# High parts first, low parts after, and the gate loads of layer 0's second attention released from VectorE's order: a two-layer attention trunk

## The chip, the cores and the metric

The kernel runs on one core of one Trainium2 chip. The metric is the device time of one launch in microseconds, the median of three runs. Five engines work side by side, each through its own queue in order: PE (TensorE: matmuls and transposes), DVE (VectorE), ACT (ScalarE), POOL (GpSimd) and SP (SyncE, which here only issues transfers). PEld is PE's loading of weights. Lines such as L575 are line numbers of the kernel before; the changed kernel has two or three lines more above most of them, so its L577 is the same statement.

## What is computed

Two layers of a trunk with two kinds of attention side by side. 512 latent tokens and 256 context tokens, 1024 channels, heads of 64 channels. One layer, cut to what matters:

```
h    = rmsnorm(x) * (1 + scale) + shift            # scale, shift, gate from c @ w_ada
a_k, a_v, b_k, b_v, a_q, b_q, a_z, b_z, g_a, g_b = split(h @ w_in)
a    = neighbourhood_attention(norm(a_q), norm(a_k), a_v)        # 8 heads, "NA"
b    = grouped_query_attention(rope(norm(b_q)), rope(norm(b_k)), b_v)  # 8 heads, 2 of keys, "GQA"
o_a  = (a * silu(a_z)) @ w_o_a
o_b  = (b * silu(b_z)) @ w_o_b
x    = x + gate * ((sigmoid(g_a) * o_a + sigmoid(g_b) * o_b) @ w_out)
```

Both attentions also read the context's keys. Layer 0 updates the context tokens as well; layer 1, the last, does not.

## The kernel before

**Products in three terms.** Weights and activations are float32. Each is split into a high part (a rounded copy, made by ACT) and a low part (the original minus the high part, made by DVE or POOL), and every projection is high x high + low x high + high x low, three matmuls (L467 to L469). A weight's way is therefore: a load on SP (`raw`), ACT's cast (`whi`, L452), and a subtraction (`wlo`, L454) on DVE or, by turns, on POOL.

**Queries.** A block of 128 tokens of queries is projected, normalised per head (`y`, L549), and turned on PE by four transposes into a bank of PSUM (`pst`, L561). `turn` then reads the turned block twice per half: ACT writes the high part in float16, DVE the low part. The halves are the two heads of a pair (partitions 0 to 63 and 64 to 127); for the neighbourhood attention's queries (`qa`, scaled by a column of gains: L574 on ACT, L575 on DVE) the first and the fourth block are also cut in two along the tokens, so such a block has four pairs of copies and the others have two. The grouped attention's queries (`qb`) are turned without gains (L571 on ACT, L572 on DVE). In program order each pair is high, low, high, low.

**Attention.** `pipeline` goes over eight heads: scores of head h (`pss`), on DVE the sum with the bias and the maximum (L1018 for NA, L1206 for GQA), on ACT the exponential, a split of the weights into two float16 parts (`h`: ACT L895, DVE or POOL L896), a transpose by transfer on SP (`ht`, L900; for the context's own queries `ct`), then the values of head h-1 on PE (`psv`, `pst`).

**Fill.** PE's remaining work in the attention is pieces of projections from a list, `fill`: gate projections (`psf` banks, evacuated by ACT and DVE: `za` and `zt` at L667) and then the output projection of the first branch, whose activations are split into `gah` (ACT, L711) and `gal` (POOL, L712) and whose results go into `tg` by DVE (L747). The list comes from `in_order`: the loads of two chunks first, then each chunk's pieces, with the load of the chunk after next behind the first ones. In layer 0's GQA the call passes `first`, which is true in layer 0, and every later load of that list is then issued through `tied`:

```
def tied(fn):
    behind(ON_DVE, fn, latest(ON_DVE, 4))
...
fill = in_order(gates[n_na:] + o_chunks("a", prepare, evac_a), first)
```

`behind` adds orders without a semaphore: the DVE instructions that the load emits may not be placed before the last four DVE instructions emitted until then.

**What sets the order.** The program is written in one order, and a list scheduler, which simulates the engines and transfers, places each instruction on its engine. So the order of an engine's queue differs from that of the text, and a changed dependency can move things far from it.

## Time and profile before

| | |
|---|---|
| runs | 1122.0, 1124.23, 1125.29 us; median 1124.23 us |
| the profiled execution | 1119.77 us, of which the span that the profile covers is 1118.0 us |
| granted clock of PE, mean | 0.992 |
| transfers | 178.21 MB, 159 GB/s in the mean |

The profile gives each engine's busy time, groups of instructions, waits, and the instructions in order of time. A window's row lists for each engine its busy time and, in brackets, how many instructions it had, then the clock granted to PE (1.00 is full) and the share of the transfer engines. Times are microseconds from the span's start. Layer 0's query blocks of NA lie at 120 to 160 us, its NA at 160 to 300, its query blocks of GQA at 345 to 375 and its GQA at 375 to 540; layer 1's NA queries and NA lie at 745 to 868 and its GQA after that.

### The profile page before, as it was taken

What the parts mean: (1) busy time and instruction counts of PE and PEld (TensorE: products, weight loads), DVE (VectorE), ACT (ScalarE), POOL (GpSimd) and SP (SyncE); (2) the same over time, 40 slices, a digit from 0 to 9 for tenths busy, and PEclk for the clock granted to TensorE, in tenths of its full rate; (3) what the DMA queues carried; (4) which work ended last, traced back from release to release, by engine and by line L of the source; (5) the groups of instructions that cost most, each with busy time, mean ns of one, the idle gap of its engine ahead of it and who ended that gap; (6) DMA issues with size and microseconds to landing.
All of it is one profiled execution on the core that took longest, in us unless ns stands there. A gap on an engine that the chain in (4) does not pass through costs nothing.

```text
span 1118.0 us, 16953 instructions
## 1 busy us (share of the span) xinstructions
PE 1073.3 (96%) x5672; PEld 842.5 (75%) x5672; DVE 785.9 (70%) x1667; ACT 607.5 (54%) x1219; POOL 454.3 (41%) x393
## 2 busy tenths in 40 slices
PE   8999999999999999889999999999999998999898
PEld 5688877878887867666888778887766986756587
DVE  4667999975379488657576776486886775677473
ACT  6465458776433566666231275644888436688221
POOL 1044324654246155465322534332445453575421
PEclk9999999999999999989999999999999999999999
DMA  8565335654543499789533643753645537789543
GB/s 358 207 175 173 95 109 114 139 131 100 176 125 123 127 217 211 161 208 245 178 103 115 198 123 95 216 170 108 159 112 122 157 102 192 189 231 233 143 143 94
DMA packets 244463, 178.21 MB, mean 159 GB/s; under 512 B 160284, under 2 KB 210328, under 8 KB 242712
## 3 DMA queue, kind: packets, MB, share of 16 engines
q1 hardware_dynamic: 236896, 162.61, 53.6%
q0 software_dynamic: 2368, 7.87, 2.2%
q10 hardware_dynamic: 5112, 6.66, 2.1%
q8 instruction: 45, 0.74, 0.3%
q14 instruction: 42, 0.34, 0.1%
HBM read 118.86 MB, written 20.47 MB: 125 GB/s over the span
## 4 chain that ended last, share of the span: by engine, by line
PE 42%; issue 6%; DVE 6%; DMA 6%; ACT 4%; POOL 2%; SPq 1%; DVEq 0%; POOLq 0%; ACTq 0%
PE psx L468 7%; PE psx L469 7%; PE psx L467 7%; PE psf L467 5%; PE psf L468 4%; PE psf L469 4%; DMA ht<-h 3%; PE pst L1223 1%; PE pst L1224 1%; DMA rawb<-in_w_ada_dram 1%; PE pss L925 1%; PE pss L926 1%; ACT p L1207 1%; ACT h L895 1%; DVE p L1206 1%
## 5 line engine op out<-in xcount | busy, mean ns | idle before, releaser
L896 POOL TENSOR_TENSOR h<-p,h 128x256 f16<-128x256 f32 (+2 forms) x104 | 107.8, 1044 | 156.6 <-ACT h L895 106.9
L454 POOL TENSOR_TENSOR wlo<-raw,whi 128x512 fp32r<-128x512 f32 x70 | 98.5, 1415 | 118.8 <-ACT whi L452 87.6
L467 PE MATMUL psf<-hx,whi 128*128 128x512 f32 (+1 forms) x360 | 139.5, 387 | 2.8 <-DVE za L667 2.2
L469 PE MATMUL psf<-hx,wlo 128*128 128x512 f32 (+1 forms) x360 | 137.8, 383 | 0.0
L468 PE MATMUL psf<-hx,whi 128*128 128x512 f32 (+1 forms) x360 | 137.3, 381 | 0.0
L468 PE MATMUL psx<-wlo,hx 128*128 128x512 f32 (+1 forms) x328 | 120.8, 369 | 1.3 <-DVE wlo L440 1.3
L467 PE MATMUL psx<-whi,hx 128*128 128x512 f32 (+1 forms) x328 | 120.9, 370 | 0.0
L469 PE MATMUL psx<-whi,hx 128*128 128x512 f32 (+1 forms) x328 | 120.3, 367 | 0.0
L440 POOL TENSOR_TENSOR wlo<-raw,whi 128x512 fp32r<-128x512 f32 x40 | 54.4, 1362 | 136.9 <-ACT whi L437 98.4
L452 ACT CAST whi<-raw 128x512 fp32r<-128x512 f32 x136 | 81.1, 619 | 52.2 <-DMA raw<-in_w_in_dram 25.1
L437 ACT CAST whi<-raw 128x512 fp32r<-128x512 f32 x88 | 53.9, 624 | 92.1 <-PE psx L469 30.8
L540 POOL TENSOR_TENSOR ss<-ss,ehalf 128x8 f32<-128x8 f32 (+2 forms) x40 | 65.1, 1632 | 87.8 <-DVE ss L537 86.4
L1207 ACT ACTIVATE p<-pss,mx,vb 128x768 f32<-128x768 f32 x64 | 63.4, 992 | 44.8 <-DVE mx L1206 44.4
L1206 DVE CUSTOM_DVE_ANT_0 p<-pss,vb 128x768 f32<-128x768 f32 x64 | 64.3, 1013 | 31.8 <-PE pss L926 27.0
L895 ACT CAST h<-p 128x256 f16<-128x256 f32 (+2 forms) x136 | 81.6, 617 | 7.3 <-DVE p L854 2.9
L454 DVE TENSOR_TENSOR wlo<-raw,whi 128x512 fp32r<-128x512 f32 x66 | 70.8, 1079 | 20.6 <-ACT whi L452 19.3
L467 PEld LDWEIGHTS psf<-hx,whi 128*128 128x128 f32 x360 | 68.4, 190 | 15.3 <-DVE za L667 2.4
L469 PEld LDWEIGHTS psf<-hx,wlo 128*128 128x128 f32 x360 | 68.2, 189 | 12.0
L468 PEld LDWEIGHTS psf<-hx,whi 128*128 128x128 f32 x360 | 68.3, 190 | 11.3
L468 PEld LDWEIGHTS psx<-wlo,hx 128*128 128x128 f32 x328 | 62.0, 189 | 11.9 <-DVE wlo L440 2.2
L469 PE MATMUL psx<-hx,wlo 128*128 128x256 f32 (+1 forms) x208 | 69.5, 334 | 0.7 <-DVE wlo L454 0.7
L469 PEld LDWEIGHTS psx<-whi,hx 128*128 128x128 f32 x328 | 61.9, 189 | 10.1 <-DVE hx L383 0.4
(350 smaller groups left out, 2900.7 us busy)
## 6 DMA issues: line engine op xcount, KB each, us to landing
raw<-in_w_in_dram SPq DMA_DIRECT2D x168, 256.0 KB, 3.1
rawb<-in_w_ada_dram SPq DMA_DIRECT2D x48, 256.0 KB, 2.9
raw<-in_w_out_dram SPq DMA_DIRECT2D x32, 256.0 KB, 3.0
tg<-gs SPq DMA_DIRECT2D x4, 1536.0 KB, 7.3
rawx<-in_w_ada_dram SPq DMA_DIRECT2D x4, 1024.0 KB, 11.3
rawy<-in_w_ada_dram SPq DMA_DIRECT2D x4, 1024.0 KB, 10.5
gs<-zt ACTq DMA_DIRECT2D x16, 256.0 KB, 2.6
raw<-in_w_o_a_dram SPq DMA_DIRECT2D x16, 256.0 KB, 3.4
```

The source lines that it names most:

```text
L437: S.copy(hi[:, :n], raw[:, :n])
L440: e.tensor_tensor(lo[:, :n], raw[:, :n], F(hi[:, :n]), ALU.subtract)
L452: S.copy(hi, raw)
L454: lo_eng(i).tensor_tensor(lo, raw, F(hi), ALU.subtract)
L467: T.matmul(ps, lhs[0], rhs[0], start=first, stop=False)
L468: T.matmul(ps, lhs[0], rhs[1], start=False, stop=False)
L469: T.matmul(ps, lhs[1], rhs[0], start=False, stop=last)
L540: G.tensor_tensor(ss, ss, ehalf[:, :n], ALU.pow)
L895: S.copy(h[:, 0], p[:, :n])
L896: eng.tensor_tensor(h[:, 1], p[:, :n], h[:, 0], ALU.subtract)
L1206: V.tensor_tensor_reduce(p, pss, lift, gq_ndq, 3e38, ALU.add, ALU.min, mx[:, 0:1])
L1207: S.activation(p, pss, AF.Exp, bias=mx[:, 0:1], scale=gq_dq, accum_out=r[:, i:i + 1])
```

## The change

Two edits. In `turn` the low part is no longer issued right behind its high part: the subtractions are put into a list, `todo`, and issued when all the high parts of the block have been. And the call of `in_order` for the GQA's fill no longer passes `first`, so in layer 0, too, its loads are issued without `tied`.

```
+        todo = []
+
         def pair(hi, lo, x, g):
             if g is None:
                 S.copy(hi, x)
-                V.tensor_tensor(lo, x, hi, ALU.subtract)
+                todo.append(lambda: V.tensor_tensor(lo, x, hi, ALU.subtract))
             else:
                 S.activation(hi, x, AF.Copy, scale=g)
-                V.scalar_tensor_tensor(lo, x, g, hi, ALU.mult, ALU.subtract)
+                todo.append(lambda: V.scalar_tensor_tensor(lo, x, g, hi, ALU.mult, ALU.subtract))
...
                 pair(d[own], d[other], x[own], None if g is None else g[own])
+        run(todo, len(todo))
...
-            fill = in_order(gates[n_na:] + o_chunks("a", prepare, evac_a), first)
+            fill = in_order(gates[n_na:] + o_chunks("a", prepare, evac_a))
```

The instructions are the same ones and as many on every engine; only places change. Three of them follow, each before and then after. The first number in a name tells buffers apart.

DVE in layer 0's GQA, at about 392 us. Before (`mx_837` is a maximum of the context's queries, `wlo_846` and `wlo_852` are low parts of gate weights, `p_864` is the next scores' pass, `r_839` a reciprocal that PE turns next):

```order
L938 TENSOR_REDUCE mx_837_4333<-pss_836_4328 128x2
L940 TENSOR_SCALAR mx_837_4333<-mx_837_4333,vb_659_3447 128x2
L454 TENSOR_TENSOR wlo_846_4354<-raw_844_4350,whi_845_4352 128x512
L454 TENSOR_TENSOR wlo_852_4366<-raw_850_4362,whi_851_4364 128x512
L1206 ISA p_864_4487,mx_865_4488<-pss_863_4482,vb_659_3447 128x768
L1206 ISA mx_865_4488 128x1
L905 RECIPROCAL r_839_4337<-r_839_4337 128x2
L908 SCALAR_TENSOR_TENSOR zb_800_4122<-pst_889_4559,vb_659_3447,zb_800_4122 64x512
L908 SCALAR_TENSOR_TENSOR zb_800_4122<-psv_892_4583,vb_659_3447,zb_800_4122 64x256
L1206 ISA p_868_4501,mx_869_4502<-pss_867_4496,vb_659_3447 128x768
```

After:

```order
L941 TENSOR_REDUCE mx_837_4333<-pss_836_4328 128x2
L943 TENSOR_SCALAR mx_837_4333<-mx_837_4333,vb_659_3447 128x2
L1209 ISA p_864_4487,mx_865_4488<-pss_863_4482,vb_659_3447 128x768
L1209 ISA mx_865_4488 128x1
L908 RECIPROCAL r_839_4337<-r_839_4337 128x2
L454 TENSOR_TENSOR wlo_899_4606<-raw_897_4602,whi_898_4604 128x512
L911 SCALAR_TENSOR_TENSOR zb_800_4122<-pst_889_4559,vb_659_3447,zb_800_4122 64x512
L911 SCALAR_TENSOR_TENSOR zb_800_4122<-psv_892_4583,vb_659_3447,zb_800_4122 64x256
L454 TENSOR_TENSOR wlo_905_4618<-raw_903_4614,whi_904_4616 128x512
L1209 ISA p_868_4501,mx_869_4502<-pss_867_4496,vb_659_3447 128x768
```

`wlo_846` and `wlo_852` now stand 19 rows further ahead, before the first scores' pass of the stage, and the next two low parts, `wlo_899` and `wlo_905`, have come forward to this place.

DVE where the output projection of the first branch begins, at about 486 to 496 us. Before (`ho_1086` empties the bank that `psv_1123` is turned into, `tg_1053` takes in the projection's bank `psf_1055`):

```order
L908 SCALAR_TENSOR_TENSOR zb_800_4122<-pst_1120_5655,vb_659_3447,zb_800_4122 64x512
L883 TENSOR_TENSOR ho_1086_5513<-psv_1085_5504,ho_1086_5513 64x256
L908 SCALAR_TENSOR_TENSOR zb_800_4122<-psv_1123_5679,vb_659_3447,zb_800_4122 64x256
L896 TENSOR_TENSOR h_1102_5596<-p_1100_5592,h_1102_5596 128x768
L1206 ISA p_1104_5605,mx_1105_5606<-pss_1103_5600,vb_659_3447 128x768
L1206 ISA mx_1105_5606 128x1
L747 SCALAR_TENSOR_TENSOR tg_1053_5363<-tg_1053_5363,psf_1055_5367 128x512
```

After:

```order
L911 SCALAR_TENSOR_TENSOR zb_800_4122<-pst_1120_5655,vb_659_3447,zb_800_4122 64x512
L454 TENSOR_TENSOR wlo_1093_5541<-raw_1091_5537,whi_1092_5539 128x512
L1209 ISA p_1104_5605,mx_1105_5606<-pss_1103_5600,vb_659_3447 128x768
L1209 ISA mx_1105_5606 128x1
L454 TENSOR_TENSOR wlo_1131_5716<-raw_1129_5712,whi_1130_5714 128x512
L886 TENSOR_TENSOR ho_1086_5513<-psv_1085_5504,ho_1086_5513 64x256
L911 SCALAR_TENSOR_TENSOR zb_800_4122<-psv_1123_5679,vb_659_3447,zb_800_4122 64x256
L899 TENSOR_TENSOR h_1102_5596<-p_1100_5592,h_1102_5596 128x768
L1209 ISA p_1108_5618,mx_1109_5619<-pss_1107_5613,vb_659_3447 128x768
L1209 ISA mx_1109_5619 128x1
L750 SCALAR_TENSOR_TENSOR tg_1053_5363<-tg_1053_5363,psf_1055_5367 128x512
```

Two low parts that stood after the projection's first banks now stand ahead of `ho_1086`; the pass `p_1104` has come forward, and `tg_1053` stands behind one more pass, `p_1108`. On PE the scores that follow `p_1104` in the same bank (`pss_1111`) and the next ones (`pss_1115`) have come forward to stand before the second bank, `psf_1056`; on POOL `h_1081` has come forward to stand before the four `gal` subtractions.

SP at the end of layer 1's NA, at about 848 to 866 us. Before (`h_17..` up to `h_1797` are head 6's weights to be transposed, `h_1823` to `h_1838` head 7's; `raw_18..` are loads of the next stage's weights, of which three can be open at a time):

```order
L900 DMA_TRANSPOSE ht_1559_7952<-h_1782_8872 128x4x64 x2
L669 DMA gs0_87<-zt_1848_9162 128x512
L449 DMA raw_1878_9307<-in_w_in_dram 128x2x256
L435 DMA raw_1881_9313<-in_w_in_dram 128x512
L900 DMA_TRANSPOSE ht_1559_7952<-h_1787_8888 128x4x128
L900 DMA_TRANSPOSE ht_1559_7952<-h_1792_8903 128x4x128
L900 DMA_TRANSPOSE ht_1559_7952<-h_1797_8918 128x4x128
L900 DMA_TRANSPOSE ht_1559_7952<-h_1823_9026 128x4x64 x2
```

After:

```order
L993 DMA bint_1557_7946<-b_int1_84 128x256
L995 DMA bedg_1558_7947<-b_edge1_86 64x128
L672 DMA gs0_87<-zt_1846_9134 128x512
L449 DMA raw_1878_9307<-in_w_in_dram 128x2x256
L435 DMA raw_1881_9313<-in_w_in_dram 128x512
L435 DMA raw_1884_9319<-in_w_in_dram 128x512
L672 DMA gs0_87<-zt_1848_9162 128x512
L435 DMA raw_1887_9325<-in_w_in_dram 128x512
L900 DMA_TRANSPOSE ht_1559_7952<-h_1823_9026 128x4x64 x2
```

All of head 6's transposes now stand ahead of head 7's bias (`bint`, `bedg`), and two more loads, `raw_1884` and `raw_1887`, which followed head 7's transposes before, stand ahead of them.

## The prediction

> **What bounds the kernel now.** I read the page first, then windows by stage, then PE's waits in the touched stages, and last the instructions in order of time around each.

> ```profile
> PE 1073.3 (96%) x5672; PEld 842.5 (75%) x5672; DVE 785.9 (70%) x1667; ACT 607.5 (54%) x1219; POOL 454.3 (41%) x393
> ```

> PE is busy for 1073.3 of the span's 1118.0 us, so nothing that ACT or DVE saves counts unless PE waited for it. PE's idle 44.7 us are the first bound. The change leaves the instructions as they are and touches four stages; their windows (after the range: its length, then busy time and count of PE, PEld, DVE, ACT, POOL, the granted clock, transfers):

> ```profile
> 120.00:160.00 40.00, 37.76 (x193) 31.39 (x192) 37.59 (x85) 14.86 (x27) 9.72 (x6) 0.96 0.33 95
> 345.00:375.00 30.00, 29.39 (x158) 24.56 (x157) 22.02 (x35) 13.39 (x24) 13.16 (x8) 1.00 0.38 118
> 375.00:540.00 165.00, 153.22 (x871) 114.36 (x870) 115.41 (x205) 105.20 (x199) 82.57 (x56) 0.98 0.82 191
> 745.00:868.00 123.00, 118.35 (x610) 88.18 (x609) 94.71 (x255) 84.30 (x187) 51.58 (x54) 1.00 0.51 127
> ```

> PE idles there for 2.2, 0.6, 11.8 and 4.7 us, 19.3 in all. What it waited for in the first, third and fourth (us in total, times, longest):

> ```profile
> PE psf L467 <- DVE za L667: 2.2, 1, 2.2
> ```

> ```profile
> PE psf L467 <- DVE tg L747: 5.0, 4, 2.9
> PE psv L960 <- DMA ct<-h: 2.9, 1, 2.9
> PE psv L907 <- DVE r L905: 1.2, 1, 1.2
> ```

> ```profile
> PE psv L1039 <- issue: 1.3, 1, 1.3
> PE pss L1039 <- issue: 0.8, 1, 0.8
> PE psx L469 <- DVE wlo L454: 0.7, 1, 0.7
> ```

> None of these is a wait for a turned query. But a gap has a second price: the clock. Windows of 3.41 us, in pairs around three gaps:

> ```profile
> 942.62:946.03 3.41, 1.61 (x12) 1.12 (x11) 2.96 (x6) 1.91 (x4) 0.00 (x0) 1.00 1.15 298
> 946.03:949.45 3.42, 2.85 (x14) 1.32 (x14) 0.00 (x0) 1.43 (x4) 1.64 (x1) 1.00 0.66 172
> 143.90:147.31 3.41, 1.17 (x9) 0.93 (x8) 3.31 (x8) 2.03 (x5) 0.00 (x0) 1.00 0.63 196
> 147.31:150.72 3.41, 3.41 (x10) 2.63 (x9) 3.27 (x10) 0.68 (x1) 0.00 (x0) 0.50 0.76 232
> ...
> 492.06:495.47 3.41, 1.42 (x5) 0.50 (x4) 3.37 (x2) 0.00 (x0) 3.41 (x3) 1.00 0.93 371
> 495.47:498.88 3.41, 2.27 (x10) 2.28 (x11) 2.02 (x5) 2.73 (x5) 0.73 (x1) 0.50 1.04 167
> 498.88:502.29 3.41, 3.41 (x12) 2.38 (x11) 2.42 (x5) 1.92 (x4) 2.05 (x2) 0.50 1.15 81
> ```

> **Part 1, high parts first.** What it takes away can be read from the two tiles (busy ones: minimum, median, maximum in ns; then the reasons for which the engine sat idle, us and times):

> ```profile
> L575 DVE SCALAR_TENSOR_TENSOR qa<-pst,gcol,qa x28: 476/490/756, 122.5 to 779.3; 64x256 f16<-64x256 f32 x16, 64x512 f16<-64x512 f32 x12
> ...
>   DVE qa L575: 27.9, 15
> ```

> ```profile
>   DVE qb L572: 13.5, 9
> ...
>   PE pst L561: 0.4, 1
> ```

> ACT's high copy waited for DVE's low part of the half before, 27.9 and 13.5 us in all. That is ACT's idleness: PE waited for the turned `qb` 0.4 us once. I cost these 41 us at nothing. PE hides them, since a turned block is needed only when attention begins; without that cover they would cost at most what the last block of a stage waited. The second stage (`qb`) has 0.6 us of PE idle in 30, so it gives 0, at most 0.6 either way.

> In layer 0's `qa` blocks DVE is the queue (37.59 of 40 us), so order there matters:

> ```profile
> 146.87 0.50 PE L467 MATMUL psf<-hx,whi 128*128 128x512 f32 x1 [2.24 <-DVE za L667]
> ...
> 151.99 0.60 PE L561 MATMUL pst<-ident,y 128*128 128x128 f32 x4
> ```

> PE's 2.24 us end with `za`, which in the new order has one low more and one statistics pass less ahead of it, about the same time. But the last block's four transposes move from 151.99 into this gap (0.60 us in the row, whose end is modelled: I take 0.4). Idle in the window falls to 1.84 us, near the 1.80 after which the clock stayed, so I count the 1.7 us as saved. Against that, that block's second low (0.76, the longest in the tile's row) now stands ahead of the next `za` on DVE, and PE's next bank waits for it: +0.8. Sum -0.4 - 1.7 + 0.8 = **-1.3**, and +0.4 if the clock falls after all.

> In layer 1 the same regrouping puts the first scores 29 matmuls further ahead on PE, some 5 us at this stage's mean (118.35 us for 610), and shifts fill to the back; PE's work stays. To gain are the three waits quoted, 2.8 us; I take **-0.7**, the one for `wlo`, since the two at the end wait for transposes on a queue that is full:

> ```profile
> 854.26 10.33 SPq L900 DMA_TRANSPOSE ht<-h  x8
> ```

> Eight in 10.33 us are 1.3 each, back to back. Heads start sooner, but two loads now stand ahead of head 7's five (first rival).

> **Part 2, the untied loads.** The low parts leave a place where PE waits:

> ```profile
> 379.81 1.02 DVE L1206 CUSTOM_DVE_ANT_0 p<-pss,vb 128x768 f32<-128x768 f32 x1 [9.22 <-PE pss L926]
> ...
> 393.49 2.36 DVE L454 TENSOR_TENSOR wlo<-raw,whi 128x512 fp32r<-128x512 f32 x2
> ...
> 396.71 0.15 DVE L905 RECIPROCAL r<-r 128x2 f32<-128x2 f32 x1
> ```

> ```profile
> 396.92 0.43 PE L907 MATMUL psv<-ident,r 128*128 128x128 f32 x2 [1.25 <-DVE r L905]
> ```

> `wlo_846` and `wlo_852` go into the 9.22 us in which DVE idles before 379.81; without their 2.36 us the reciprocal comes before PE asks for it, so 1.1 of 1.25 us go. Two later low parts take their place behind the reciprocal, and DVE is then as late as before: part of the gain is handed back at the wait for `ct` (2.9 us), at the end of a chain through DVE and SP. I keep half, **-0.6** (bounds -1.1 and 0). The loads behind them are issued sooner too, on SP ahead of some transposes; an issue holds SP for less than one of the transposes above, and I count it inside that half.

> Then the start of the output projection, the largest gap:

> ```profile
> 489.68 0.42 DVE L883 TENSOR_TENSOR ho<-psv,ho 64x256 f32<-64x256 f32 x1 [2.69 <-ACT ho L882]
> ...
> 491.96 2.93 DVE L896 TENSOR_TENSOR h<-p,h 128x768 f16<-128x768 f32 x1
> ...
> 495.87 0.68 DVE L747 SCALAR_TENSOR_TENSOR tg<-tg,psf 128x512 f32<-128x512 f32 x1
> ```

> ```profile
> 485.79 7.16 POOL L712 TENSOR_TENSOR gal<-za,gah 128x768 fp32r<-128x768 f32 x4
> 492.92 1.16 POOL L896 TENSOR_TENSOR h<-p,h 128x512 f16<-128x512 f32 x1
> ```

> ```profile
> 493.00 0.50 PE L468 MATMUL psf<-gal,whi 128*128 128x512 f32 x1 [0.26 <-POOL gal L712]
> ...
> 496.61 0.58 PE L467 MATMUL psf<-gah,whi 128*128 128x256 f32 x1 [2.87 <-DVE tg L747]
> ```

> ```profile
> L454 DVE TENSOR_TENSOR wlo<-raw,whi x12: 671/828/2597, 393.5 to 539.5; 128x512 fp32r<-128x512 f32 x12
> ```

> ```profile
> L452 ACT CAST whi<-raw 128x512 fp32r<-128x512 f32 x136 | 81.1, 619 | 52.2 <-DMA raw<-in_w_in_dram 25.1
> ```

> For: `p_1104` runs sooner, in DVE's 2.69 us of idleness, and frees the bank for the scores that now stand ahead of `psf_1056`. PE does two sets of scores in the gap; a set is two matmuls of 512 and two of 256 columns, at most 1.5 us by the 0.50 for 512 in the row at 493.00; as matmuls overlap I take 0.5 a set, 1.0 us. The idle 2.87 + 0.26 becomes about 2.1, spread over two windows, neither with 1.8: the clock stays, 2.8 us more. Against: `h_1081` (1.16) ahead of `gal`, with its cast on ACT (0.6, as the cast of as many columns in the last row), makes the fourth `gal` 1.8 us late, and two low parts stand before `ho_1086`; at the median 0.83 they fit into the 2.69 us. These two delays overlap; I charge 1.8. Sum -1.0 - 2.8 + 1.8 = **-2.0**. Bounds: -3.8, if the delays are hidden too; +2.5 if the low parts take 2.6 us each and the clock falls again.

> The row's spread matters here: an extreme of 2.6 us against 0.67, and in 492.06:495.47, with POOL busy throughout, `h` took 2.93. [...]

> **Sum.** -1.3 - 0.7 - 0.6 - 2.0 = -4.6 us: 1115.2 against the profiled execution's 1119.77 (span 1118.0 and 1.8 around it). That execution lies 4.5 us below the median of 1124.23; taking the difference over as it is gives 1119.6, 0.41% less. A measurement of this kernel can tell about 0.3%, 3.4 us, from no change.

> **Rivals.**

> 1. Slower: SP at the end of layer 1's NA. `raw_1887` needs the buffer of `raw_1878`, three loads before, and until that is split SP issues nothing, so head 7's five transposes wait.

> ```profile
> raw<-in_w_in_dram SPq DMA_DIRECT2D x168, 256.0 KB, 3.1
> ```

> Landing 3.1, cast 0.6, low part 0.8 by the rows above: 4.5 us. It decides if head 7's weights are ready before that load is split; for it speaks that SP was full there, against it that the heads start some 5 us sooner. If so, PE's last wait grows from 1.3 by 4.5, with 28 matmuls less of fill before it to cover that, and the clock falls once, 1.7: +6.2 in place of -0.7. The total is +2.3, 1126.5; with the clock not won at the two other places it is +6.8, 1131.0. Chance 0.21.

> 2. No difference: the two gaps stay long enough for the clock to fall. Then part 1 gives +0.4, the projection's start +0.8, the rest -1.3: -0.1, 1124.1. [...] Chance 0.26.

> 3. More: the waits at layer 1's end go as well (-2.8), `ct` hands nothing back (-1.1), the delays at the projection are hidden (-3.8): -9.0, 1115.2. Chance 0.10.

> The forecast has the remaining 0.43. The range takes in rival 3 with 2 us more and rival 1 without its worst end: 1113 to 1129.5. Faster by over 0.3%: the forecast and rival 3, less a part of the forecast that comes out just short, 0.45. Within: 0.30. Slower: 0.25, rival 1 and a part of rival 2 with low parts at 2.6 us.

> **What would show it.** Right: at 397 no wait for `r`; at 456 a wait for `ct` within 1 us of 2.9; the window behind `za`'s gap at 1.00; the low parts near 487 to 491 at under 1.3 us each; PE's gap before `psf_1056` under 2 us and the clock at 1.00 there; layer 1's last wait under 2 us. Wrong: a new PE gap over 2 us with a window at 0.50 behind it, above all at the end of layer 1's NA, or a time over 1124.

## The result: slower by half a per cent, and the profile after

The changed kernel took 1127.49 us (median of ten runs, 1125.61 to 1132.15) against 1122.3 us for the kernel before beside it (1119.21 to 1125.29): a ratio of 1.005, 95% interval 1.0032 to 1.0068. It is slower by about 5.2 us. The two profiled executions lie 9.1 us apart (1128.9 us with a span of 1127.1, against 1119.77 with 1118.0); that overstates it, since the one of before lies below its own median and the one of after above its own. So a difference between the two traces counts below only where other runs repeat it.

The page of the changed kernel, first line of its first part:

```profile
PE 1074.9 (95%) x5672; PEld 841.7 (75%) x5672; DVE 789.6 (70%) x1667; ACT 607.7 (54%) x1219; POOL 451.7 (40%) x393
```

PE did the same work (1074.9 us against 1073.3). Its idle time grew from 44.7 us to 52.2. The windows of the touched stages, columns as in the prediction:

```profile
120.00:160.00 40.00, 36.63 (x194) 30.40 (x193) 38.43 (x86) 13.82 (x26) 10.35 (x6) 1.00 0.31 91
345.00:375.00 30.00, 29.81 (x164) 25.42 (x163) 23.94 (x37) 13.60 (x24) 13.92 (x9) 1.00 0.36 111
375.00:540.00 165.00, 149.95 (x846) 110.92 (x845) 112.48 (x199) 103.47 (x196) 73.58 (x54) 0.97 0.79 191
745.00:868.00 123.00, 117.21 (x593) 86.14 (x592) 98.69 (x259) 82.03 (x184) 50.70 (x52) 1.00 0.49 125
```

Two stages lost: layer 0's GQA, where PE idles for 15.1 us in place of 11.8, and layer 1's NA, which got through 593 matmuls in 123 us in place of 610. PE's waits in the first of them, at 375 to 545 us (us in total, times, longest):

```profile
PE psv L910 <- DVE ho L886: 6.8, 1, 6.8
PE psv L963 <- DMA ct<-h: 2.6, 1, 2.6
```

and in layer 1's NA, at 745 to 878 us:

```profile
PE pss L928 <- DVE qa L577: 1.7, 1, 1.7
PE psv L1042 <- DMA ht<-h: 1.4, 1, 1.4
```

The first row of each is a wait that the kernel before did not have. The 6.8 us is at the start of the output projection. VectorE there (start, duration, then the idle time before it and its releaser):

```profile
487.97 9.04 DVE L454 TENSOR_TENSOR wlo<-raw,whi 128x512 fp32r<-128x512 f32 x1 [0.70 <-ACT whi L452]
497.04 1.02 DVE L1209 CUSTOM_DVE_ANT_0 p<-pss,vb 128x768 f32<-128x768 f32 x1
...
497.98 0.69 DVE L454 TENSOR_TENSOR wlo<-raw,whi 128x512 fp32r<-128x512 f32 x1
498.58 0.41 DVE L886 TENSOR_TENSOR ho<-psv,ho 64x256 f32<-64x256 f32 x1
```

GpSimd in the same stretch:

```profile
486.99 1.16 POOL L899 TENSOR_TENSOR h<-p,h 128x512 f16<-128x512 f32 x1
488.11 7.13 POOL L715 TENSOR_TENSOR gal<-za,gah 128x768 fp32r<-128x768 f32 x4
495.20 1.25 POOL L454 TENSOR_TENSOR wlo<-raw,whi 128x512 fp32r<-128x512 f32 x1
```

and PE:

```profile
487.89 0.38 PE L1226 MATMUL pst<-ht,vb 128*128 128x512 f16 x1 [1.51 <-DVE zb L911]
...
499.05 0.69 PE L910 MATMUL psv<-ident,r 128*128 128x128 f32 x2 [6.82 <-DVE ho L886]
```

One low part (`wlo_1093`) is on VectorE for 9.04 us; its twin ten us later needs 0.69. It begins during GpSimd's `h`, and ends 0.56 us after the last of the six GpSimd instructions that run without a break (495.20 + 1.25 = 496.45). `ho_1086` behind it is late by as much, and PE, which turns into the bank that `ho` empties, stands still for 6.82 us. The clock follows:

```profile
488.51:491.92 3.41, 3.41 (x17) 1.82 (x16) 3.41 (x1) 2.19 (x5) 3.41 (x3) 1.00 0.95 383
491.92:495.34 3.42, 0.31 (x3) 0.03 (x1) 3.42 (x1) 0.00 (x0) 3.42 (x3) 1.00 1.05 392
495.34:498.75 3.41, 0.00 (x0) 0.00 (x0) 3.38 (x5) 0.59 (x1) 1.11 (x1) 0.50 1.00 273
498.75:502.17 3.42, 3.12 (x10) 2.14 (x11) 2.57 (x4) 1.94 (x4) 2.07 (x2) 0.50 0.01 2
```

`psf` matmuls of 512 columns at a granted 0.50 started 0.43 us apart in the kernel before (148.39, 148.81), against 0.23 at 1.00 (151.08, 151.31). So about half of the 3.12 us in the last window, 1.6, is lost to the clock; before, 2.8 us were lost at this place. So the new loss is the wait and not the clock.

### The profile page after: what moved, and what is told of

It reads as the page before. It is cut to its first block, busy times and chain, and to the rows that moved or that the text cites. A ratio compares the mean times of both kernels' runs of the same rounds, so it can differ in the third digit from the quotient of the medians.

```text
span 1127.1 us, 16974 instructions
## 1 busy us (share of the span) xinstructions
PE 1074.9 (95%) x5672; PEld 841.7 (75%) x5672; DVE 789.6 (70%) x1667; ACT 607.7 (54%) x1219; POOL 451.7 (40%) x393
## 5 line engine op out<-in xcount | busy, mean ns | idle before, releaser
L899 POOL TENSOR_TENSOR h<-p,h 128x256 f16<-128x256 f32 (+2 forms) x104 | 110.5, 1068 | 164.4 <-ACT h L898 137.1
L467 PE MATMUL psf<-hx,whi 128*128 128x512 f32 (+1 forms) x360 | 139.3, 387 | 4.3 <-DVE za L670 2.2
L454 POOL TENSOR_TENSOR wlo<-raw,whi 128x512 fp32r<-128x512 f32 x70 | 97.2, 1396 | 106.2 <-ACT whi L452 59.7
L469 PE MATMUL psf<-hx,wlo 128*128 128x512 f32 (+1 forms) x360 | 137.3, 381 | 0.0
L468 PE MATMUL psf<-hx,whi 128*128 128x512 f32 (+1 forms) x360 | 136.9, 380 | 0.0
L468 PE MATMUL psx<-wlo,hx 128*128 128x512 f32 (+1 forms) x328 | 120.9, 369 | 1.3 <-DVE wlo L440 1.3
L467 PE MATMUL psx<-whi,hx 128*128 128x512 f32 (+1 forms) x328 | 120.9, 371 | 0.0
L469 PE MATMUL psx<-whi,hx 128*128 128x512 f32 (+1 forms) x328 | 120.4, 367 | 0.0
L452 ACT CAST whi<-raw 128x512 fp32r<-128x512 f32 x136 | 80.8, 619 | 54.2 <-DMA raw<-in_w_in_dram 31.7
L454 DVE TENSOR_TENSOR wlo<-raw,whi 128x512 fp32r<-128x512 f32 x66 | 77.2, 1175 | 23.0 <-ACT whi L452 22.8
L467 PEld LDWEIGHTS psf<-hx,whi 128*128 128x128 f32 x360 | 68.0, 189 | 17.6 <-DVE za L670 2.6
L469 PEld LDWEIGHTS psf<-hx,wlo 128*128 128x128 f32 x360 | 68.0, 189 | 12.3
L468 PEld LDWEIGHTS psf<-hx,whi 128*128 128x128 f32 x360 | 68.1, 189 | 11.2
L468 PEld LDWEIGHTS psx<-wlo,hx 128*128 128x128 f32 x328 | 62.0, 189 | 11.9 <-DVE wlo L440 2.2
L467 PE MATMUL psx<-hx,whi 128*128 128x256 f32 (+1 forms) x208 | 69.3, 333 | 0.4 <-DVE za L670 0.4
L469 PEld LDWEIGHTS psx<-whi,hx 128*128 128x128 f32 x328 | 61.9, 189 | 10.1 <-DVE hx L383 0.4
## 6 DMA issues: line engine op xcount, KB each, us to landing
raw<-in_w_in_dram SPq DMA_DIRECT2D x168, 256.0 KB, 3.0
rawb<-in_w_ada_dram SPq DMA_DIRECT2D x48, 256.0 KB, 2.8
raw<-in_w_out_dram SPq DMA_DIRECT2D x32, 256.0 KB, 3.0
gs<-zt ACTq DMA_DIRECT2D x16, 256.0 KB, 2.5
raw<-in_w_o_a_dram SPq DMA_DIRECT2D x16, 256.0 KB, 3.4
```

The costliest lines, as they stand in the source:

```text
L452: S.copy(hi, raw)
L454: lo_eng(i).tensor_tensor(lo, raw, F(hi), ALU.subtract)
L467: T.matmul(ps, lhs[0], rhs[0], start=first, stop=False)
L468: T.matmul(ps, lhs[0], rhs[1], start=False, stop=False)
L469: T.matmul(ps, lhs[1], rhs[0], start=False, stop=last)
L899: eng.tensor_tensor(h[:, 1], p[:, :n], h[:, 0], ALU.subtract)
```

## The experiments

Each was run against the kernel before on the same chip; ratios carry 95% intervals. For all of them the same matmuls were found in the trace by their names, and the table gives how many us later than in the trace of before they start (the time in before names the place). Two stretches tell most: 485 to 508 us (the start of layer 0's output projection) and 765 to 944 us (layer 1's NA, from just before its first scores, and what follows it).

| kernel | ratio | at 485 | at 508 | at 765 | at 944 | first stretch | second |
|---|---|---|---|---|---|---|---|
| the change | 1.0050 | 0.3 | 4.8 | 4.2 | 8.3 | +4.5 | +4.1 |
| e1 loads untied only | 1.0021 | 0.8 | 5.7 | 5.5 | 6.9 | +4.9 | +1.4 |
| e2 high parts first only | 1.0036 | 2.7 | 1.8 | 2.2 | 6.9 | -0.8 | +4.7 |
| e3 output loads tied | 1.0014 | 1.5 | 0.7 | 1.5 | 4.2 | -0.9 | +2.7 |
| e5 untied, `gal` on VectorE | 0.9958 | 2.8 | 1.8 | -2.9 | -3.0 | -1.0 | -0.1 |
| e6 first edit, layer 0 | 1.0000 | 2.0 | 2.0 | 1.4 | 1.5 | -0.1 | +0.1 |
| e7 first edit, layer 1 | 1.0031 | 3.4 | 2.6 | 1.1 | 4.3 | -0.9 | +3.2 |
| e8 e7, loads behind transposes | 1.0039 | 2.4 | 2.3 | 2.0 | 5.5 | -0.1 | +3.5 |
| e9 both edits, `gal` on VectorE | 0.9965 | 2.7 | 0.9 | -2.6 | 1.0 | -1.9 | +3.6 |
| e10 only `gal` on VectorE | 0.9934 | -0.3 | -4.2 | -4.2 | -4.7 | -3.9 | -0.5 |
| e11 layer 1, first three blocks | 1.0010 | 4.0 | 3.0 | 2.7 | 4.8 | -1.0 | +2.1 |
| e12 layer 1, fourth block | 0.9993 | 1.1 | 1.1 | -0.2 | 1.1 | 0.0 | +1.3 |
| e13 untied, half of `gal` | 0.9972 | 2.6 | 5.1 | 0.9 | 1.0 | +2.5 | +0.1 |
| e14 e9, fourth block in pairs | 0.9941 | 1.9 | 0.1 | -4.3 | -1.9 | -1.9 | +2.4 |
| e15 `gal` on VectorE, both layers | 0.9926 | 1.1 | -2.7 | -5.7 | -5.8 | -3.9 | -0.1 |

The scatter of the second stretch in kernels whose layer 1 queries are as before (e1, e5, e6, e10, e13, e15) is -0.5 to +1.4. Each row is one execution. Where `gal` is on VectorE the scheduler also mixes attention and fill in another order from 486 to 680 us, so the column at 508 depends there on the matmul taken (e5: -1.0 to 4.8 between 506 and 512 us); the column at 765, where the orders agree again, does not.

**e1, the second edit alone.** `turn` as before, and the call of `in_order` as in the change:

```
-            fill = in_order(gates[n_na:] + o_chunks("a", prepare, evac_a), first)
+            fill = in_order(gates[n_na:] + o_chunks("a", prepare, evac_a))
```

> Only the second edit: layer 0's GQA loads untied, high and low parts alternating as before. Theory A (the low part wlo_1093 is starved on VectorE while POOL does its four gal subtractions back to back, 9 us, and PE waits 6.8 us for the reciprocal's turn behind it): slower than before by about 4 us (0.35%), one VectorE L454 instruction of over 7 us near 490 us and a PE gap of over 5 us behind it. Theory B (the whole loss comes from SP's queue at the end of layer 1's NA): no difference from before, within 1 us. Theory C (nothing but the order on VectorE counts, two more instructions of normal length ahead of the reciprocal): a gap of 3 to 4 us in place of 2.9, under 2 us lost.

1124.39 us, ratio 1.0021 (1.0008 to 1.0034): 2.4 us slower (0.9 to 3.8), less than the +4.9 of the first stretch in its one trace. PE waits 6.9 us. The long subtraction is there again to the hundredth:

```profile
488.54 9.04 DVE L454 TENSOR_TENSOR wlo<-raw,whi 128x512 fp32r<-128x512 f32 x1 [0.70 <-ACT whi L452]
```

**e2, the first edit alone.** `turn` as in the change, `in_order(..., first)` as before.

> Only the first edit: high parts first, then low parts; the loads of layer 0's GQA tied as before. Theory A: the part of the loss that lies in layer 1's NA, 1 to 3 us (0.1 to 0.3%), with SP idle for some us ahead of head 7's transposes; no VectorE L454 instruction over 3 us near 490. Theory B: the whole loss, about 5 us. If the first edit is harmless and the layer 1 loss was chance: within 1 us of before.

1125.88 us, ratio 1.0036 (1.0012 to 1.006). Nothing is lost at the projection and 4.7 us in layer 1's stretch. The two ratios together make 1.0057, and the change measured 1.005, as it would if the edits lose separately.

**e3, the change with the output projection's loads tied.** The gate chunks' loads stay untied:

```
-        def in_order(chunks, tie=False):
+        def in_order(chunks, tie=99):
...
-                    res.append((lambda ld=ld: tied(ld)) if tie else ld)
+                    res.append((lambda ld=ld: tied(ld)) if i + 2 >= tie else ld)
...
+            fill = in_order(..., len(gates[n_na:]) if first else 99)
```

> The changed kernel, but the loads of the first branch's output projection are tied behind VectorE as before; only the gates' loads stay untied. Theory A: wlo_1093 goes back behind the projection's first banks, the 9 us instruction and the 6.8 us gap go, and 4 us come back: about 1123 to 1124 against 1127.5 for the change, that is 1 to 2 us slower than before. Theory B: stays about 5 us slower than before. Theory C: 1 to 2 us come back.

1123.64 us, ratio 1.0014 (0.9996 to 1.0032). The place is as it was in the kernel before: the window at 484 to 510 us has 21.81 us of PE work, against 17.43 in the change and 22.27 before.

```profile
484.00:510.00 26.00, 21.81 (x124) 16.04 (x123) 17.30 (x29) 18.61 (x37) 19.64 (x15) 0.93 0.93 245
```

So of the loads it is those of the output projection whose low parts did the harm; tying them again gives back 0.36%, 4.0 us, of the change's 0.5%.

**e4, a probe of the held subtraction.** Behind the end of the kernel before, GpSimd does 0, 1, 2 or 4 subtractions of `gal`'s form and VectorE one of `wlo`'s form, both released by the same instruction; then the same with an operand in PSUM, and with a copy in float16.

```
for n, what in ((0, 0), (1, 0), (2, 0), (4, 0), (0, 1), (4, 1), (0, 2), (4, 2)):
    G.tensor_tensor(tok, prev, now, ALU.add)
    for i in range(n):
        G.tensor_tensor(gout[i], src, F(ghi), ALU.subtract)
    if what == 0:
        V.tensor_tensor(lo, raw, F(phi), ALU.subtract)
...
```

> The kernel before with a probe behind its end: VectorE's subtraction of 512 columns from SBUF (the form of wlo) beside 0, 1, 2 and 4 POOL subtractions of 768 columns back to back (the form of gal, 1.8 us each), then VectorE's product with one operand in PSUM beside 0 and 4, then its float16 copy beside 0 and 4. Theory A (VectorE gets no turn while POOL goes on without a pause): the subtraction takes 0.7, about 2.4, about 4.2 and about 7.7 us. Sharing (half speed while POOL runs): 0.7, 1.4, 1.4, 1.4. A fixed extreme as before's longest row: none over 2.6. The product from PSUM and the copy tell whether the form counts: unslowed, or as long as the subtraction.

VectorE with none, one and four of them (with two it is the same 2.27); the last two rows are the product with an operand in PSUM, beside none and four:

```profile
1123.81 0.69 DVE L1358 TENSOR_TENSOR plo<-praw,pwhi 128x512 fp32r<-128x512 f32 x1 [0.31 <-POOL ptok L1353]
1124.82 2.27 DVE L1358 TENSOR_TENSOR plo<-praw,pwhi 128x512 fp32r<-128x512 f32 x1 [0.31 <-POOL ptok L1353]
...
1131.52 2.27 DVE L1358 TENSOR_TENSOR plo<-praw,pwhi 128x512 fp32r<-128x512 f32 x1 [1.85 <-POOL ptok L1353]
1139.15 0.69 DVE L1360 TENSOR_TENSOR pyy<-psf,praw 128x512 f32<-128x512 f32 x1 [5.36 <-POOL ptok L1353]
1140.16 0.69 DVE L1360 TENSOR_TENSOR pyy<-psf,praw 128x512 f32<-128x512 f32 x1 [0.31 <-POOL ptok L1353]
```

The subtraction takes 2.27 us in place of 0.69 beside one GpSimd instruction, which itself takes 1.80 us, and no longer beside two (4.01 us) or four (7.52 us); the product with one operand in PSUM takes 0.69 us beside four as beside none. So the probe shows a wait, but not the long one: the expectation that it lasts as long as the row (Theory A) missed here, and the three times fit "none over 2.6".

**e5, untied loads and `gal` on VectorE.** e1 with layer 0's four subtractions moved:

```
-            hilo(za, gated["a"], range(4))
+            hilo(za, gated["a"], range(4), V if first else G)
```

> Only the second edit, and in layer 0 the four gal subtractions of the first branch are made by VectorE in place of POOL, so that POOL has no long run beside wlo_1093. The probe said that VectorE's two-input subtraction waits for POOL (2.27 us beside one POOL instruction), but went in behind the first of several. Theory A (POOL's run holds wlo_1093 back): it takes 0.7 to 1.3 us, the PE gap of 6.9 us ahead of the reciprocal's turn shrinks to under 3.5 us although VectorE has 4 us more work there; 2 to 4 us less than with the second edit alone (1124.4). Theory C (the place in VectorE's order alone): the gap stays at 6 us or more.

1116.26 us, ratio 0.9958 (0.9937 to 0.9979). The low part that took 9.04 us takes 0.68, PE's longest wait there is 2.4 us, and the first stretch goes from +4.9 to -1.0. That it is faster than the kernel before says more than the theory did, and e10 shows that this part isn't due to the loads.

**e6, the first edit in layer 0 only**; the low parts of layer 1's blocks are issued right behind each high part (`now = hp["l"] != 0`).

> High parts first in layer 0 only; loads tied as before; layer 1 as before. Theory D (the first edit's loss lies in layer 1, in SP's queue ahead of head 7): within 1 us of before. Theory E (it lies in layer 0, where the last block's low parts now stand ahead of the key copies and the next za on VectorE and PE waits 1 to 2 us at 154 to 158 us): 1 to 3 us slower.

1121.24 us, ratio 1.0000 (0.9974 to 1.0027). In layer 0 alone no gain and no loss can be told.

**e7, the first edit in layer 1 only** (`now = hp["l"] != 1`).

> High parts first in layer 1 only; loads tied as before. Theory D: slower by 3 to 4 us (0.3%), all of it between 770 and 875 us, and SP idle for 4 to 6 us ahead of head 7's five transposes. Theory E: within 1 us of before.

1124.39 us, ratio 1.0031 (1.0006 to 1.0056), +3.2 us in the second stretch. The first edit's loss is in layer 1.

**e8, e7 with the next stage's first weights ordered behind head 7's last transpose on SP.**

```
+            turned_last = [i.name for i in nc.cur_bb.bb.instructions
+                           if i.engine == ON_SP and "ranspose" in type(i).__name__][-1:]
...
-                behind(ON_ACT, load_q, tails)
+                behind(ON_SP, lambda: behind(ON_ACT, load_q, tails), turned_last)
```

> As the run with high parts first in layer 1 only, but the next stage's query weights are ordered on SP behind head 7's last transpose, so that raw_1884 and raw_1887 no longer stand ahead of the five. Theory D (SP's order, the prediction's first rival): PE's last wait of the stage stays under 1.5 us and the stage ends 2.5 to 3.5 us sooner than without that order; near before or up to 1 us faster. If the loss of layer 1 comes from scores and fill in another order on PE: no change against that run.

1124.45 us, ratio 1.0039 (1.0014 to 1.0064). In e7, as in the changed kernel, SP does what the first rival said; here is its queue:

```profile
855.64 0.92 SPq L435 DMA_DIRECT2D raw<-in_w_in_dram  x2
...
861.85 0.33 SPq L435 DMA_DIRECT2D raw<-in_w_in_dram  x1
862.50 6.39 SPq L909 DMA_TRANSPOSE ht<-h  x5
```

And in e8:

```profile
863.87 6.40 SPq L909 DMA_TRANSPOSE ht<-h  x5
...
870.99 1.34 SPq L435 DMA_DIRECT2D raw<-in_w_in_dram  x3
```

With the three loads (L435) behind them, the five transposes start no sooner: 863.87 is 1.4 us later than in e7, of which 0.9 was there at 765 already. PE waits as long for the last transposes (1.3 us against 1.4) and the stretch is +3.5 (e7: +3.2). The theory that this queue makes layer 1 slow falls.

**e9, both edits, `gal` on VectorE in layer 0.**

> The changed kernel with layer 0's four subtractions gal on VectorE instead of GpSimd. If the change's loss is two separate things, the low part held on VectorE behind GpSimd's gal (about 5 us with the clock) and layer 1's regrouped queries (about 3.5 us), the first goes and the second stays: the product of the ratios measured apart is 0.9958 x 1.0031 = 0.9989, about 1119.5 us, within 0.996 to 1.002, and the long gap of 6.8 us before psf's second bank falls under 3 us. If the two edits hinder each other instead, so that the regrouped queries bring the loss back somewhere else, it stays at 1.004 or more, about 1125 us.

1117.26 us, ratio 0.9965 (0.9943 to 0.9987), within what separate losses give. PE's longest wait at the projection is 1.5 us, the first stretch is -1.9 and the second still +3.6.

**e10, the kernel before with only `gal` on VectorE.**

> The kernel before, loads tied as they were, with only layer 0's four subtractions gal on VectorE. If what made the untied loads with gal on VectorE faster (0.9958) needed both, this one gives 1.000, within 0.998 to 1.002: VectorE then does some 4.5 us more work at a place where it is not the only one that PE waits for. If the whole gain comes from taking gal off GpSimd, it gives 0.996, about 1117 us, and untying the loads is worth nothing.

1114.04 us, ratio 0.9934 (0.9909 to 0.996): the rival was right, the gain comes from taking `gal` off GpSimd. Its window at 484 to 510 us:

```profile
484.00:510.00 26.00, 22.72 (x131) 16.51 (x129) 21.68 (x36) 17.81 (x34) 11.11 (x10) 1.00 1.06 292
```

PE's idle time is 3.3 us against 3.7 before, and the clock 1.00 against 0.87: the long gap has become short ones and no longer halves the clock. In this trace 2 us of the gain are handed back by 600 us and won again at 650 to 672, where the order differs and PE's waits (3.7 us at 540 to 680) shrink to 2.1. So how much of the 0.66% comes from GpSimd's shorter row and how much from the new order that the scheduler finds for it is not shown. It corrects the reading of e5: moving `gal` gains as much with tied loads (0.66%) as with untied ones (1.0021 to 0.9958, 0.63%), and untying gains nothing in either case.

**e11 and e12, the first edit in parts of layer 1**: all blocks but the fourth (`now = hp["l"] != 1 or t == 3`), and the fourth alone (`t != 3`). The fourth block is cut in two and has four low parts.

> High parts first in layer 1's blocks of queries, except for the fourth block, which keeps its pairs; loads tied as before. The first head's scores then stand where they stood before (29 matmuls later than in the changed kernel). Theory: layer 1's loss comes from the fourth block, whose four low parts go last together and whose scores are put so near behind them that PE waits 1.7 us and has its fill in another order: without it 1.000, within 0.998 to 1.002, and no wait of PE for qa. Rival: the regrouping costs in every block, or by shifting VectorE's other work: 1.003, as with all four blocks.

> High parts first in the fourth block of layer 1's queries alone; loads tied as before. The first head's scores stand 29 matmuls sooner, as in the changed kernel. Theory (the fourth block and the sooner scores are the loss): 1.003, within 1.001 to 1.005, PE waits 1.5 to 2 us for qa before the first scores, and the stretch of layer 1's NA takes 2.5 to 3.5 us more. Rival (the other three blocks are the loss): 1.000 and no such stretch.

e11: 1122.55 us, ratio 1.001 (0.9986 to 1.0033), second stretch +2.1, no wait for `qa`. PE waits for `za` instead, just before the first scores. On VectorE:

```profile
771.18 4.37 DVE L926 COPY kk<-ka 64x1536 f16<-64x1536 f16 x4
775.58 0.69 DVE L676 SCALAR_TENSOR_TENSOR za<-za,psx 128x512 f32<-128x512 f32 x1
```

on GpSimd and PE:

```profile
771.14 2.86 POOL L454 TENSOR_TENSOR wlo<-raw,whi 128x512 fp32r<-128x512 f32 x2 [10.98 <-ACT whi L452]
```

```profile
776.32 0.50 PE L467 MATMUL psx<-hx,whi 128*128 128x512 f32 x1 [1.52 <-DVE za L676]
```

In the kernel before, the same `za` runs ahead of the copies of the keys (`kk`), and PE does not wait for it:

```profile
767.18 0.69 DVE L667 SCALAR_TENSOR_TENSOR za<-za,psx 128x512 f32<-128x512 f32 x1
...
768.79 1.71 DVE L917 COPY kk<-ka 64x1536 f16<-64x1536 f16 x3
```

With the other three blocks regrouped, `za` stands behind four of these copies. A copy takes 0.57 us before; in e11 two of the four run beside GpSimd's two `wlo`, and the four take 4.37 us. It is the form that the probe found held (0.55 alone, 2.14 beside GpSimd).

e12: 1119.84 us, ratio 0.9993 (0.9972 to 1.0014), second stretch +1.3, within the scatter, though its first scores wait as they do in the change:

```profile
775.40 0.23 PE L934 MATMUL pss<-kk,qa 128*128 128x128 f16 x1 [1.70 <-DVE qa L578]
```

So the fourth block alone does not bring the loss, and the wait of 1.7 us for `qa` does not explain it: the theory of e12 falls. The theory of e11 holds by the time, but its interval reaches 1.003, the rival's value, and in the trace the other three blocks cost more than the scatter.

**e13, untied loads with two of the four `gal` on VectorE and two on GpSimd.**

```
-            hilo(za, gated["a"], range(4))
+            hilo(za, gated["a"], (0, 2), V if first else G)
+            hilo(za, gated["a"], (1, 3))
```

> Loads untied, and of layer 0's four subtractions gal two on VectorE and two on GpSimd. If the low part on VectorE is held as long as GpSimd's row of work lasts without a break, two gal of 1.8 us fewer shorten the hold from 9.0 to about 5.4 us (less if the row is cut by waits), PE's gap of 6.9 falls to 3.5 to 4.5 us, and the time lies between those of none and of all four on VectorE: 0.998 to 1.001, about 1120 us. If it is held for one instruction at most when its turn comes (the probe behind the kernel's end: 2.27 us), the hold is under 2.8 us and the time is near that with all four on VectorE, 0.996.

1118.67 us, ratio 0.9972 (0.9954 to 0.999), between all and none, a little below the range expected. The low part itself takes 0.86 us now, and PE's longest wait is 2.6 us in place of the 3.5 to 4.5 expected. On VectorE it is the second `gal` that is held:

```profile
489.84 5.77 DVE L715 TENSOR_TENSOR gal<-za,gah 128x768 fp32r<-128x768 f32 x1
...
496.43 0.86 DVE L454 TENSOR_TENSOR wlo<-raw,whi 128x512 fp32r<-128x512 f32 x1
```

and GpSimd's row is shorter by two:

```profile
488.13 1.97 POOL L891 TENSOR_TENSOR zb<-zb,ho 64x512 f32<-64x512 f32 x1
490.07 1.15 POOL L900 TENSOR_TENSOR h<-p,h 128x512 f16<-128x512 f32 x1
491.19 3.60 POOL L715 TENSOR_TENSOR gal<-za,gah 128x768 fp32r<-128x768 f32 x2
494.76 1.98 POOL L454 TENSOR_TENSOR wlo<-raw,whi 128x512 fp32r<-128x512 f32 x1
```

5.77 us, where 5.4 was expected for the low part. VectorE's `gal` ended at 495.61, 0.82 us behind GpSimd's last (494.79), and GpSimd's `wlo` next to it took 1.98 us, against 1.25 in the change. So in these two cases the hold is the shorter for the shorter row of `gal` (5.77 us with two of them, 9.04 with four), and it is no property of that one low part.

**e14, e9 with layer 1's fourth block in pairs as before** (`now = hp["l"] == 1 and t == 3`).

> Both edits, layer 0's gal on VectorE, and layer 1's fourth block of queries (and of the grouped attention's) with its low parts in pairs as before. Beside the same kernel with the fourth block regrouped (0.9965; layer 1's neighbourhood attention 2.9 us longer than in the kernel before): if the fourth block together with the others makes that stretch long, it falls to within 0.5 us of before and the time goes to 0.994, about 1114.5 us. If the stretch stays 2.5 us or more longer, the other three blocks do it, and the time stays at 0.9965.

1115.81 us, ratio 0.9941 (0.9917 to 0.9965), second stretch +2.4 in place of e9's +3.6. The time is what the first theory expected (0.994), but the two ratios' intervals overlap, and the trace does not bear it out. The expectation counts from 773 us, and from there it is +0.5 against +2.9; but by 773 PE has already waited 1.5 us for `za`, as in e11. So in these two traces the fourth block's pairs take away 1.2 us of the 3.6, and 2.4 stay with the other three blocks.

**e15, the kernel before with `gal` on VectorE in both layers.**

> The kernel before with the gal subtractions on VectorE in layer 1 too. Layer 1's start of the output projection has a gap of PE of about 2.8 us behind GpSimd's work at 1044 and h of 3.39 us on VectorE at 1034; if taking gal off GpSimd helps there as in layer 0 (4 us), 0.990, about 1110 us. If GpSimd's work there isn't what PE waits for, it stays at 0.9934, and VectorE's added 3 us (four of 0.7) may cost up to 0.002.

1113.87 us, ratio 0.9926 (0.99 to 0.9952). Against e10's 0.9934 no difference can be told, and the interval takes in both expectations: whether layer 1's projection gains is not shown.

## Why the prediction was wrong, step by step

**Start of the output projection, forecast -2.0, measured +4.5 (e1: +4.9).** This is the step that failed: "two low parts stand before `ho_1086`; at the median 0.83 they fit into the 2.69 us". The place was right and the order was right; the price was the wrong row. Of the two low parts the second took 0.69 and the first 9.04. Even the bound (2.6 each, +2.5 in all) was too small. I took the longest instance of the tile; it had itself been held to the end of a GpSimd row, one much shorter than `gal`'s:

```profile
522.78 3.76 POOL L454 TENSOR_TENSOR wlo<-raw,whi 128x512 fp32r<-128x512 f32 x3
```

```profile
524.49 2.60 DVE L454 TENSOR_TENSOR wlo<-raw,whi 128x512 fp32r<-128x512 f32 x1
```

It began in the second of the three and ended 0.55 us after the last (522.78 + 3.76 = 526.54). The row that should have set the bound was quoted beside it: `gal` x4 at 7.16 us without a break, over exactly the time in which the two low parts were to run. Both gains counted there (scores in the gap, clock kept) went with it: the gap grew, and two windows were granted 0.50, as before. The runs show 0.69 us grown to 2.27 beside GpSimd in the probe and to 9.04 in the change, over six GpSimd instructions. The prediction quoted a row of that kind, `h` at 2.93 us with GpSimd busy throughout, and priced the low parts by their median all the same.

**Layer 1's regrouping, forecast -0.7, measured +4.1 (2.7 to 4.7 in six kernels with all four blocks regrouped).** The wait for `wlo` went as said, the last wait stayed (1.3 before, 1.4 after), and a new one of 1.7 us came: the first scores, 29 matmuls further ahead, now wait for the fourth block's low parts, which go last. I had costed sooner heads at nothing. That wait is not the whole of it, since e12 has it and its stretch is no longer than that of e1, whose layer 1 is as before. A second wait came from the other three blocks, for `za` behind the held key copies: 1.5 us in e11 and e14, 0.4 with all four. What is shown: the loss is in layer 1 (e6, e7), and it isn't SP's queue (e8). In the traces the larger part (+2.1 of e7's 3.2, +2.4 of e9's 3.6) stays when the fourth block keeps its pairs (e11, e14), and the times are too close to decide. Only 2.4 of the change's 4.1 us are idle time of PE (8.1 us between the matmuls at 765 and at 944, against 5.7); how the rest comes about stays open.

**Layer 0's `qa` blocks, forecast -1.3; no difference that the runs can tell** (e6, 1.0000, 0.9974 to 1.0027). The half-speed window went as said, and of the gap of 2.24 us more than was said: its window idles for 0.24 us, where 1.84 was forecast, and the one from 147.31 was granted 1.00:

```profile
143.90:147.31 3.41, 3.17 (x18) 2.50 (x17) 3.33 (x8) 1.75 (x3) 0.00 (x0) 1.00 0.49 166
147.31:150.72 3.41, 3.41 (x18) 2.87 (x17) 3.35 (x9) 0.10 (x1) 0.00 (x0) 1.00 0.75 221
```

By 150 us the matched matmuls have gained 3.6 us. But the same VectorE work, still a queue of 38.4 us in 40, was then late twice more, and by 160 us all of that is gone:

```profile
154.06 0.22 PE L928 MATMUL pss<-kk,qa 128*128 128x128 f16 x1 [1.21 <-DVE kk L920]
158.02 0.50 PE L467 MATMUL psf<-hx,whi 128*128 128x512 f32 x1 [1.92 <-DVE za L670]
```

I charged 0.8 for the second low ahead of the next `za`; it was 1.92, and the wait for `kk` wasn't in the sum. **The second stage, `qb`, forecast 0:** PE idles 0.2 us in 30, right.

**The gap at 397, forecast -0.6.** No wait for `r`, as said, but 1.32 us for `zt` in its place. By 453 us 0.8 us had been gained; by 458 it was handed back. The wait for `ct` was no longer than before (2.6 against 2.9, right within 1 us), but behind it the clock fell, as it did not in the kernel before. Two windows of the change, then of before:

```profile
450.97:454.38 3.41, 1.48 (x11) 0.92 (x10) 1.86 (x4) 3.41 (x8) 1.83 (x2) 1.00 0.86 219
454.38:457.79 3.41, 2.78 (x10) 1.82 (x11) 3.38 (x5) 1.68 (x3) 2.97 (x2) 0.50 1.09 246
```

```profile
451.07:454.48 3.41, 2.16 (x17) 1.59 (x15) 1.83 (x5) 3.41 (x9) 1.28 (x1) 1.00 0.61 141
454.48:457.89 3.41, 1.78 (x11) 1.38 (x12) 3.38 (x6) 1.72 (x5) 3.19 (x2) 1.00 1.07 274
```

The change's wait leaves 1.93 us idle in one window; before's is split, 1.25 and 1.63. The window is lost in all nine traces with one of the edits in layer 0 and in three of the eight without, so chance has a part in it. Half handed back was forecast; all of it was, by a term that was not in the sum.

**The rivals.** The first rival's two loads did stand ahead of head 7's transposes, but these would have started no sooner without them (e8); the time landed in its range for other reasons. The second rival was right that the clock falls again at the projection (two windows at 0.50), and wrong at 147 us (1.00). The third is out: neither `ct` nor the waits at layer 1's end were won. The range, 1113 to 1129.5, held 1127.49 by luck: only through the slower rival's room, whose mechanism was not the one that acted.

## What to carry to other kernels

Before a subtraction of two SBUF operands is moved on VectorE, look at what GpSimd does at that time, and price it, at worst, by the length of GpSimd's unbroken row, not by the median of its own kind (here 9.04 us beside a row that had 8.48 us to run, where the median was 0.83; the probe's product with one operand in PSUM took its 0.69 us beside four). Where GpSimd's row lies at a point that PE waits for, moving that row to VectorE can be worth more than the order around it (here 0.66%, without either edit of the change). A reorder that brings consumers forward also uses up the work that covered their inputs: count the new first waits (here 1.7 us for `qa`, up to 1.5 for `za`) as well as the one removed.

## What was not expected of the hardware

A VectorE instruction with two operands in SBUF took 9.04 us beside six GpSimd instructions in the change (the one running when it began included) and 5.77 us beside four in e13, where their like took 0.69 (`wlo` at 497.98 us in the change) and 0.95 (`gal` at 487.17 us in e10). The first ended behind the end of the row, the second behind the last `gal` in it. The held subtractions of 512 columns whose GpSimd row is shown here ended 0.55 or 0.56 us after the end of a GpSimd instruction (in the change, in the probe beside one and at 524.49 us in the kernel before). Yet in the probe the subtraction took no more than 2.27 us, beside one, two or four. A product with an operand in PSUM took its 0.69 us beside four, and a float16 copy 2.14 (0.55 alone). What decides between 2.27 us and 9.04 was not found. On GpSimd, too, a `wlo` took 1.98 us right behind the row beside which VectorE's `gal` took 5.77 (e13), against 1.25 in the change.
